# A hybrid block on one core: the local attention's quarters further apart, and longer rows for the ffn's tiles fh and fl

## The chip, the cores and the metric

The kernel runs on one core of one Trainium2 chip. Time is device microseconds of one execution, the lower the better; a run's time is the time of the whole launch, and the profile's span goes from the first to the last instruction of one execution.

## The reference, cut to what matters

A block of three mixers with a feed-forward part made of retrieved experts comes first; then two layers of the form below, on 256 tokens of width 1024, in float32.

```
def hybrid_layer(x, ...):
    h = rms_norm(x, norm1_g)
    za, zb, zc, zd, zg = split(h @ w_in)
    ya = retention(za, ...)            # rotary, decayed scores, group norm
    yb = conformer_conv(zb, ...)       # 31 taps per channel, layer norm
    yc = spatial_gating(zc, ...)
    yd = swa_attention(zd, ...)        # the local attention
    mix = sum over n of sigmoid(gate n) * (y_n @ w_branch[n])
    x = x + mix @ w_out
    h = rms_norm(x, norm2_g)
    gt, up = split(h @ w_ffn_in)       # 2 x 2816 columns
    return x + (silu(gt) * up) @ w_ffn_out

def swa_attention(zd, ...):            # blocks of 128 queries, 2 kv heads, 4 q heads each
    q, k = rms_norm(...), rms_norm(...)
    s = q k^T * d**-0.5 + bias         # keys of the block and of the one before it
    m = max(max(s), sink)
    p = exp(s - m)
    o = (p / (sum(p) + exp(sink - m))) @ v
```

## The kernel before

**Weights.** Every weight matrix is cut into blocks of 128 x 128, stored in the order of use. SyncE loads 16 blocks at a time into "raw"; ScalarE rounds 8 of them to "whi" (line 90) and VectorE, or GpSimd in one stage, makes the remainder "wlo" (line 93). Eight blocks are a slot; there are three slots of each kind, so the two engines work up to three slots ahead of TensorE. A product is three matmuls a block (lines 173 to 175, or 179 to 181 where the activations are the stationary side): high by high, high by low, low by high.

**Tasks.** What is no weight product (the local attention, the retention, the convolution) is a Python generator. `blks` hands out a block and calls `tick` for every two blocks; a task that yields n goes on n slots later (four ticks to a slot). So tasks are strewn between the weight products when the program is written. From that order a planner, which simulates the engines, makes the order of each engine's queue: what was written earlier goes first where its inputs are there. Buffers of one tag (bg and mm in PSUM, four each; w2, seven; T4, thirteen) are given out in the order in which they were written. The remainders and the loads of the weights go ahead of everything else.

**A layer's mixers.** In order: the convolution's input (cc), the local attention's projections dq and dkv, then rq, rk, rv and rg of the retention, gu and gv of the spatial gating, then the four gated branches (first the local attention's, then the retention's, the gating's and the convolution's) and w_out. The convolution's 31 taps for each of four rows of channels (line 1134) run on VectorE, two to a slot, behind the newest remainder.

**The local attention** (`swa`) is four tasks, one for each block of queries n and kv head g, the two quarters with n = 0 (one block of keys) first. Each writes: the scores (line 1229) into two tiles "pss" of the pool bg, their evacuation with the bias (line 1231), maximum, sink and negation (lines 1236 to 1239, VectorE), four exponentials and that of the sink (lines 1241 and 1243, ScalarE), sum, reciprocal and division (lines 1244 to 1246, VectorE); then it yields. After that come the transposes "ptt" (line 1254, the helper's line 243) and their evacuation on ScalarE into a tile of w2 (line 1256), one more slot, and the product with the values "po" (line 1260), which is split into dh and dl (lines 186 and 187). The first branch needs dh and dl at its first product "pp", eight blocks after its start.

**The ffn.** `ffn` keeps silu(gt) * up as two tiles of 22 rows of 256 float32, fh and fl (lines 1453 and 1454). The first product (f_in) fills them, row by row, through `split` (lines 186 and 187). The second (f_out) reads them: in the first layer as the moving side of matmuls with 256 columns (lines 173 to 175, 528 of them), in the second as the stationary side of matmuls with 512 columns (lines 179 to 181, 264 of them).

Of the kernel before, what the change touches and what calls it, by code (L numbers as in the profile page):

```python
# [8 lines left out]
F32R = mybir.dt.float32r  # L9
# [10 lines left out]
P = 128  # L20
S = 256
# [21 lines left out]
FF = 22  # L43
N_BLOCKS = 5416
W_SHAPE = (-(-N_BLOCKS // 16), 128, 2048)
TAPS = 2
N_SCR = 5
LRU_PACE = 5
N_WARM = 50
# [80 lines left out]
class Core:  # L130
# [118 lines left out]
    def scr(self, name):  # L249
        return self.tp.tile([P, S], F32, tag="scr", name=name, bufs=N_SCR)  # L250

# [813 lines left out]
    def mixers(self, l):  # L1065
        tc, nc, a, ws = self.tc, self.nc, self.a, self.ws
        with ExitStack() as st:
            pa = st.enter_context(tc.tile_pool(name=f"a{l}", bufs=1))
            self.pad(pa)
            p = st.enter_context(tc.tile_pool(name=f"m{l}", bufs=1))  # L1070
# [7 lines left out]
            def T4(dt=F32):  # L1078
                return pa.tile([P, 4, S], dt, tag="t4", name="t4", bufs=13)

            def tmp(shape, tag, bufs=2, dt=F32):
                return p.tile(shape, dt, tag=tag, name=tag, bufs=bufs)
# [45 lines left out]
            def conv(bh, bl):  # L1128
                for j in range(4):
                    nc.vector.tensor_scalar(out=cy[:, j, :], in0=up[:, j, 0:S], scalar1=hw[:, j * NT:j * NT + 1],  # L1130
                                            scalar2=cb[:, j:j + 1], op0=ALU.mult, op1=ALU.add)
                    for i in range(1, NT):
                        with tc.issue_after(ws.on_vector):
                            nc.vector.scalar_tensor_tensor(out=cy[:, j, :], in0=up[:, j, i:i + S],
                                                           scalar=hw[:, j * NT + i:j * NT + i + 1], in1=cy[:, j, :],
                                                           op0=ALU.mult, op1=ALU.add)
                        if i % TAPS == 0:
                            yield 1
# [81 lines left out]
            def swa(n, g):  # L1220
                k0 = 0 if n else P
                nk = S - k0
                s = T4()
                for i in range(2):

                    ps = self.bg.tile([P, 2, nk], F32, tag="bg", name="pss")
                    rows = slice(64 * i, 64 * i + 64)
                    for j in range(2):
                        nc.tensor.matmul(ps[:, j, :], lhsT=qT[rows, 2 * g + j, n * P:n * P + P],
                                         rhs=kT[rows, g, 0:nk], start=True, stop=True)  # L1230
                    nc.vector.scalar_tensor_tensor(out=s[:, i:4:2, :nk], in0=ps, scalar=0.125,
                                                   in1=bias[:, 4 * g + i:4 * g + 4:2, k0:S],
                                                   op0=ALU.mult, op1=ALU.add)
                sm = tmp([P, 4, 4], "sm", 3)
                sk = sink[:, 4 * g:4 * g + 4]
                nc.vector.tensor_reduce(out=sm[:, 0, :], in_=s[:, :, :nk], axis=AX.X, op=ALU.max)
                nc.vector.tensor_tensor(out=sm[:, 0, :], in0=sm[:, 0, :], in1=sk, op=ALU.max)
                nc.vector.tensor_tensor(out=sm[:, 2, :], in0=sk, in1=sm[:, 0, :], op=ALU.subtract)
                nc.vector.tensor_scalar(out=sm[:, 0, :], in0=sm[:, 0, :], scalar1=-1.0, scalar2=None, op0=ALU.mult)
                for i in range(4):  # L1240
                    nc.scalar.activation(out=s[:, i, :nk], in_=s[:, i, :nk], func=AF.Exp, bias=sm[:, 0, i:i + 1],
                                         accum_out=sm[:, 1, i:i + 1])
                nc.scalar.activation(out=sm[:, 2, :], in_=sm[:, 2, :], func=AF.Exp)
                nc.vector.tensor_tensor(out=sm[:, 1, :], in0=sm[:, 1, :], in1=sm[:, 2, :], op=ALU.add)
                nc.vector.reciprocal(out=sm[:, 3, :], in_=sm[:, 1, :])
                nc.vector.tensor_tensor(out=s[:, :, :nk], in0=s[:, :, :nk],
                                        in1=sm[:, 3, :, None].to_broadcast([P, 4, nk]), op=ALU.mult)
                yield 3
                nkb = nk // P
                pts = []  # L1250
                for kb in range(nkb):
                    pt = self.bg.tile([P, 4, P], F32, tag="bg", name="ptt")
                    for i in range(4):
                        self.transpose(pt[:, i, :], s[:, i, kb * P:kb * P + P])
                    pts.append(tmp([P, 4, P], "w2", 7))
                    nc.scalar.activation(out=pts[-1], in_=pt, func=AF.Copy)
                yield 1
                po = self.bg.tile([P, 4, P], F32, tag="bg", name="po")
                for kb in range(nkb):
                    nc.tensor.matmul(po, lhsT=vd[:, kb if n else 0, g].rearrange("p a b -> p (a b)"),  # L1260
                                     rhs=pts[kb], start=kb == 0, stop=kb == nkb - 1)
                for i in range(2):
                    rows = slice(64 * i, 64 * i + 64)
                    src = po.rearrange("p (b two) q -> p b two q", two=2)[rows, :, i, :]
                    self.split(dh[rows, 2 * g:2 * g + 2, n * P:n * P + P], dl[rows, 2 * g:2 * g + 2, n * P:n * P + P],
                               src)
# [19 lines left out]
            def ev_rot(d):  # L1286
                def ev(c, ps):
                    nc.scalar.activation(out=d[:, c:c + 2, :], in_=ps, func=AF.Copy)
                    t_rot.append(self.add(rot(d[:, c:c + 2, :])))
                return ev  # L1290
            self.finish(*loads[1])
            self.proj_b(W2["rq"](l), 2, KD, hh, hl, ev_rot(rq))
            self.finish(*t_qk, *loads[0])
            t_swa = [self.add(swa(n, g), 1 + 3 * (2 * n + g)) for n in range(2) for g in range(2)]
            self.proj_b(W2["rq"](l), 4, KD, hh, hl, ev_rot(rq), c0=2)
            self.proj_b(W2["rk"](l), 4, KD, hh, hl, ev_rot(rk))
            rv = T4().rearrange("p a b -> p (a b)").rearrange("p (t c) -> p t c", t=2)
# [150 lines left out]
    def ffn(self, l):  # L1448
        tc, nc, a, ws = self.tc, self.nc, self.a, self.ws
        with ExitStack() as st:  # L1450
            p = st.enter_context(tc.tile_pool(name=f"f{l}", bufs=1))
            self.pad(p)
            fh = p.tile([P, FF, S], F32R, tag="fh", name="fh")
            fl = p.tile([P, FF, S], F32R, tag="fl", name="fl")

            def ev(c, ps):
                j = c // 2
                sg = p.tile([P, S], F32, tag="fsg", name="fsg", bufs=2)
                nc.scalar.activation(out=sg, in_=ps[:, 0, :], func=AF.Silu)
                nc.vector.tensor_tensor(out=sg, in0=sg, in1=ps[:, 1, :], op=ALU.mult)  # L1460
                self.split(fh[:, j, :], fl[:, j, :], sg)
            self.from_lead((f"f_in{l}", 0, 0), 2 * FF, ev)
            if l == 0:
                raw = [tuple(p.tile([P, S], F32R, tag=f"raw{i}", name="raw") for i in (k, 8 + k)) for k in range(KD)]
                g1 = self.pc2(1)
                acc = self.residual(("f_out0", 0, 0), FF, fh, fl, raw, g1)
                self.lead(W2["cc"](1), raw, g1, [acc], lambda ps: self.rsqrt(ps[:, 0, :]), LEAD_C)
                self.dump("x5", self.x)
            else:
                xn = p.tile([P, 2, KD, P], F32, tag="xn", name="xn")  # L1470
                for t in range(2):
                    for g in range(2):
                        pt = self.bg.tile([P, 4, P], F32, tag="bg", name="pxn")
                        for j in range(4):
                            self.transpose(pt[:, j, :], self.x[:, 4 * g + j, t * P:t * P + P])
                        nc.scalar.activation(out=xn[:, t, 4 * g:4 * g + 4, :], in_=pt, func=AF.Copy)
                for g in range(2):
                    def ev_fin(t, ps):
                        o = p.tile([P, 512], F32, tag="fo", name="fo", bufs=3)
                        nc.vector.tensor_tensor(out=o, in0=xn[:, t, 4 * g:4 * g + 4, :].rearrange("p a b -> p (a b)"),  # L1480
                                                in1=ps, op=ALU.add)
                        nc.sync.dma_start(out=self.out[0, t * P:t * P + P, g * 512:g * 512 + 512], in_=o)
                    self.proj_a(("f_out1", 0, 4 * g), FF, 4, fh, fl, ev_fin)
# [139 lines left out]
```

## Time and profile before

| | |
|---|---|
| median of 3 runs | 2127.13 us (2122.9 to 2136.53) |
| the profiled execution | 2123.62 us |
| its span | 2121.8 us |
| instructions | 41452 |
| TensorE busy | 2032.5 us, 96% |
| VectorE busy | 1680.1 us, 79% |
| ScalarE busy | 1164.8 us, 55% |
| GpSimd busy | 252.3 us, 12% |

The engines are called PE (TensorE's matmuls), PEld (its weight loads), DVE (VectorE), ACT (ScalarE), POOL (GpSimd) and SP (SyncE). Matmuls overlap, so the mean duration of one is longer than the distance from one to the next; the pace of a stretch is its length by its number of matmuls. The first layer's mixers lie at about 1180 to 1470 us of the span, its ffn at 1480 to 1650; the second layer's at about 1660 to 1945 and 1960 to 2117.

### The profile page before, as it was taken

Reading aid. Unit: us, or ns where it says so; the run is one execution under the profiler, and the core shown is the slowest. Engines: PE = TensorE matmul, PEld = TensorE weight load, DVE = VectorE, ACT = ScalarE, POOL = GpSimd, SP = SyncE. Lnnn points to the kernel's source line nnn. Section 1 sums busy time; section 2 is a strip of 40 time slices with the busy share of each in tenths; the row PEclk is TensorE's granted clock in tenths of the full one; section 3 lists DMA queues with packets and bytes.
Section 4 is the critical chain, followed back from the end, with each engine's and each line's share of the span. In section 5 each row is a group of like instructions: output and inputs, shape, how many; then the busy total and the mean of one; then the engine's idle time right before and its main releaser. Section 6 shows DMA issues by size and latency. Waiting matters only on the chain.

```text
span 2121.8 us, 41452 instructions
## 1 busy us (share of the span) xinstructions
PE 2032.5 (96%) x16818; PEld 1974.2 (93%) x16818; DVE 1680.1 (79%) x3308; ACT 1164.8 (55%) x1910; POOL 252.3 (12%) x162
## 2 busy tenths in 40 slices
PE   8978999959999999999999989999999999999999
PEld 7958999959999899999999878999999988999997
DVE  7847669998999999996556998977655898977654
ACT  6648754435555455554446656466545657466543
POOL 2101205844000000000000110210000110200000
PEclk9988999979999999999999999999999999999999
DMA  5443554525445444444555642555555643554554
GB/s 209 147 119 124 181 210 168 179 100 178 173 171 177 151 168 179 177 177 163 197 193 185 217 159 100 185 196 178 208 191 197 236 159 120 187 191 179 199 194 154
DMA packets 56923, 370.01 MB, mean 174 GB/s; under 512 B 6491, under 2 KB 10140, under 8 KB 13468
## 3 DMA queue, kind: packets, MB, share of 16 engines
q1 hardware_dynamic: 50256, 357.06, 46.9%
q10 hardware_dynamic: 6476, 10.31, 1.9%
q8 instruction: 131, 2.15, 0.4%
q14 instruction: 60, 0.49, 0.1%
HBM read 364.73 MB, written 2.62 MB: 173 GB/s over the span
## 4 chain that ended last, share of the span: by engine, by line
PE 81%; DVE 9%; issue 3%; DMA 3%; ACT 3%; POOL 1%; ACTq 0%; SPq 0%; POOLq 0%; DVEq 0%
PE mm L175 6%; PE mm L173 6%; PE mm L174 6%; PE acc L174 5%; PE pu L173 5%; PE acc L175 5%; PE acc L173 5%; PE pu L175 5%; PE pu L174 5%; PE pg L175 3%; PE pg L174 3%; PE pg L173 3%; DVE wlo L93 2%; PE mml L173 2%; PE mml L175 2%
## 5 line engine op out<-in xcount | busy, mean ns | idle before, releaser
L90 ACT ACTIVATE whi<-raw 128x1024 fp32r<-128x1024 f32 x677 | 716.9, 1060 | 764.6 <-PE acc L174 170.3
L93 DVE TENSOR_TENSOR wlo<-raw,whi 128x1024 fp32r<-128x1024 f32 x629 | 778.3, 1238 | 323.6 <-ACT whi L90 320.7
L173 PE MATMUL pu<-hh,whi 128*128 128x256 f32 x1024 | 290.5, 284 | 20.3 <-ACT whi L90 20.3
L175 PE MATMUL pu<-hh,wlo 128*128 128x256 f32 x1024 | 287.0, 280 | 3.1 <-POOL wlo L93 3.1
L174 PE MATMUL pu<-hl,whi 128*128 128x256 f32 x1024 | 286.1, 279 | 0.0
L175 PE MATMUL mm<-hh,wlo 128*128 128x256 f32 x1008 | 280.8, 279 | 5.3 <-DVE wlo L93 5.3
L173 PE MATMUL mm<-hh,whi 128*128 128x256 f32 x1008 | 281.6, 280 | 0.0
L174 PE MATMUL mm<-hl,whi 128*128 128x256 f32 x1008 | 280.3, 278 | 0.0
L174 PE MATMUL acc<-ga,whi 128*128 128x256 f32 x1000 | 267.9, 280 | 4.5 <-DVE ga L187 4.4
L175 PE MATMUL acc<-ga,wlo 128*128 128x256 f32 x1000 | 267.3, 279 | 0.0
L173 PE MATMUL acc<-ga,whi 128*128 128x256 f32 x1000 | 242.5, 281 | 5.0 <-ACT ga L186 5.0
L173 PEld LDWEIGHTS pu<-hh,whi 128*128 128x128 f32 x1024 | 194.7, 190 | 20.5 <-ACT whi L90 20.5
L173 PE MATMUL pg<-hh,whi 128*128 128x256 f32 x704 | 199.5, 283 | 12.3 <-ACT lth L552 11.7
L175 PE MATMUL pg<-hh,wlo 128*128 128x256 f32 x704 | 198.4, 282 | 0.6 <-DVE wlo L93 0.5
L175 PEld LDWEIGHTS pu<-hh,wlo 128*128 128x128 f32 x1024 | 194.3, 190 | 3.8 <-POOL wlo L93 3.8
L174 PE MATMUL pg<-hl,whi 128*128 128x256 f32 x704 | 197.7, 281 | 0.0
L175 PEld LDWEIGHTS mm<-hh,wlo 128*128 128x128 f32 x1008 | 190.3, 189 | 7.8 <-DVE wlo L93 6.7
L174 PEld LDWEIGHTS pu<-hl,whi 128*128 128x128 f32 x1024 | 194.0, 189 | 0.0
L174 PEld LDWEIGHTS acc<-ga,whi 128*128 128x128 f32 x1000 | 188.6, 189 | 5.3 <-DVE ga L187 5.3
L174 PEld LDWEIGHTS mm<-hl,whi 128*128 128x128 f32 x1008 | 190.3, 189 | 1.8 <-issue 1.6
L173 PEld LDWEIGHTS mm<-hh,whi 128*128 128x128 f32 x1008 | 190.6, 189 | 1.0 <-issue 0.8
L175 PEld LDWEIGHTS acc<-ga,wlo 128*128 128x128 f32 x1000 | 188.7, 189 | 0.0
(412 smaller groups left out, 4873.4 us busy)
## 6 DMA issues: line engine op xcount, KB each, us to landing
raw<-in_w SPq DMA_DIRECT2D x336, 1024.0 KB, 4.8
raw<-in_w SPq DMA_DIRECT2D x5, 512.0 KB, 7.6
bias<-bias_scr ACTq DMA_DIRECT2D x4, 512.0 KB, 5.4
bias_scr<-sbb ACTq DMA_DIRECT2D x4, 384.0 KB
cl<-in_cstl ACTq DMA_DIRECT2D x2, 576.0 KB, 7.4
x<-in_xT SPq DMA_DIRECT2D x4, 256.0 KB, 5.8
memt<-in_memT ACTq DMA_DIRECT2D x1, 1024.0 KB, 4.8
keys<-in_keysT ACTq DMA_DIRECT2D x1, 1024.0 KB
```

The lines of the kernel that those rows point to most:

```text
L90: self.on_scalar = nc.scalar.activation(out=hi, in_=src, func=AF.Copy).ins
L93: i = eng.tensor_tensor(out=lo, in0=src, in1=hi.bitcast(F32), op=ALU.subtract)
L173: mm(out, lhsT=wh, rhs=xh, start=start, stop=False)
L174: mm(out, lhsT=wh, rhs=xl, start=False, stop=False)
L175: mm(out, lhsT=wl, rhs=xh, start=False, stop=stop)
```

## The change

Two numbers of the local attention become names with other values. The quarters' tasks start 1, 5, 9 and 13 slots after they are added, where they started at 1, 4, 7 and 10; between the softmax and the transposes a quarter yields 5 slots, where it yielded 3. The rows of fh and fl are laid out 272 elements (1088 bytes) apart where they were 256 (1024); what is written and read is still the first 256 of each.

```
+SWA_SOFT, SWA_PACE = 5, 4
+ROW = 272
...
                 nc.vector.tensor_tensor(out=s[:, :, :nk], in0=s[:, :, :nk],
                                         in1=sm[:, 3, :, None].to_broadcast([P, 4, nk]), op=ALU.mult)
-                yield 3
+                yield SWA_SOFT
                 nkb = nk // P
...
-            t_swa = [self.add(swa(n, g), 1 + 3 * (2 * n + g)) for n in range(2) for g in range(2)]
+            t_swa = [self.add(swa(n, g), 1 + SWA_PACE * (2 * n + g)) for n in range(2) for g in range(2)]
...
-            fh = p.tile([P, FF, S], F32R, tag="fh", name="fh")
-            fl = p.tile([P, FF, S], F32R, tag="fl", name="fl")
+            fh = p.tile([P, FF, ROW], F32R, tag="fh", name="fh")[:, :, :S]
+            fl = p.tile([P, FF, ROW], F32R, tag="fl", name="fl")[:, :, :S]
```

## Rows read from the trace of the kernel before

**Rows 1.** The page, busy time, share of the span and instructions of each engine.
```profile
PE 2032.5 (96%) x16818; PEld 1974.2 (93%) x16818; DVE 1680.1 (79%) x3308; ACT 1164.8 (55%) x1910; POOL 252.3 (12%) x162
```
**Rows 2.** The page, the chain that ended last, shares of the span by engine.
```profile
PE 81%; DVE 9%; issue 3%; DMA 3%; ACT 3%; POOL 1%; ACTq 0%; SPq 0%; POOLq 0%; DVEq 0%
```
**Rows 3.** PE's waits: who for whom, us in total, times, longest.
```profile
PE ptt L243 <- DVE t L1246: 11.8, 4, 4.0
...
PE mm L175 <- DVE wlo L93: 5.3, 5, 2.0
```
**Rows 4.** The order of time on PE, first layer: start, length, count, idle before.
```profile
1239.28 0.39 PE L181 MATMUL mm<-wlo,hh 128*128 128x512 f32 x1
...
1255.28 0.63 PE L243 MATMUL ptt<-cst,t 128*128 128x128 f32 x4 [3.09 <-DVE t L1246]
1255.84 1.40 PE L1229 MATMUL pss<-kT,t 64*128 64x256 f32 x8
...
1274.50 1.94 PE L243 MATMUL ptt<-cst,t 128*128 128x128 f32 x8 [3.95 <-DVE t L1246]
...
1278.39 3.00 PE L1260 MATMUL po<-w,vd 128*128 128x512 f32 x4
...
1294.33 1.88 PE L1260 MATMUL po<-w,vd 128*128 128x512 f32 x4
...
1299.66 0.28 PE L173 MATMUL pp<-t,whi 128*128 128x256 f32 x1
```
**Rows 5.** Windows of 10 us: busy time by engine, PEclk (granted clock), DMA.
```profile
1250.00:1260.00 10.00, 6.91 (x39) 4.91 (x38) 9.92 (x20) 5.50 (x14) 0.00 (x0) 0.83 0.55 206
1270.00:1280.00 10.00, 6.05 (x23) 3.96 (x23) 6.72 (x14) 5.81 (x11) 0.00 (x0) 0.68 0.45 171
...
1750.00:1760.00 10.00, 9.40 (x38) 6.49 (x39) 6.43 (x14) 7.80 (x17) 0.00 (x0) 0.83 0.28 107
```
**Rows 6.** The order of time on DVE, the third quarter's first and last instruction.
```profile
1258.50 0.69 DVE L1231 SCALAR_TENSOR_TENSOR t<-pss,bias 128x512 f32<-128x512 f32 x1
...
1273.13 1.22 DVE L1246 TENSOR_TENSOR t<-t,sm 128x1024 f32<-128x1024 f32 x1
```
**Rows 7.** The order of time on ACT: evacuations of transposes, rv and rg.
```profile
1255.94 0.60 ACT L1256 ACTIVATE w<-ptt 128x512 f32<-128x512 f32 x1 [2.26 <-PE ptt L243]
1256.44 1.08 ACT L1300 ACTIVATE t<-mm 128x512 f32<-128x512 f32 x2
...
1277.03 0.59 ACT L1306 ACTIVATE w<-mm 128x512 f32<-128x512 f32 x1
```
**Rows 8.** Windows in which PE never waits, columns as in rows 5.
```profile
220.00:310.00 90.00, 90.00 (x766) 90.00 (x766) 61.09 (x86) 57.86 (x85) 15.85 (x15) 1.00 0.55 199
1366.00:1390.00 24.00, 24.00 (x206) 24.00 (x205) 22.35 (x34) 11.34 (x16) 7.80 (x7) 1.00 0.57 210
1402.00:1438.00 36.00, 36.00 (x320) 36.00 (x319) 26.79 (x43) 23.18 (x40) 1.49 (x2) 1.00 0.52 183
1500.00:1580.00 80.00, 80.00 (x709) 80.00 (x708) 45.72 (x60) 39.57 (x59) 0.00 (x0) 1.00 0.54 193
1582.00:1641.00 59.00, 59.00 (x523) 59.00 (x522) 33.51 (x42) 29.77 (x38) 0.00 (x0) 1.00 0.54 191
2058.00:2117.00 59.00, 59.00 (x260) 48.40 (x259) 26.53 (x24) 21.39 (x22) 0.00 (x0) 1.00 0.48 167
```
**Rows 9.** Windows of the two layers' local attention, columns as in rows 5.
```profile
1214.00:1300.00 86.00, 77.99 (x496) 66.46 (x495) 76.73 (x138) 47.61 (x89) 8.32 (x5) 0.94 0.40 148
1695.00:1776.00 81.00, 75.97 (x503) 65.79 (x502) 74.43 (x135) 48.13 (x89) 7.14 (x4) 0.98 0.43 153
```
**Rows 10.** Groups by line and shape: the remainder's writes to fl.
```profile
L187 DVE TENSOR_TENSOR fl<-fsg,fh 128x256 fp32r<-128x256 f32 x44 | 18.2, 419 | 0.1
```
**Rows 11.** The order of time on DVE: the fourth quarter's last split.
```profile
1298.62 0.43 DVE L187 TENSOR_TENSOR t<-po,t 64x256 fp32r<-64x256 f32 x1
```

## The prediction

> **What bounds the kernel now.** I read the page's busy shares first: TensorE (PE) is busy 96% of the span, VectorE (DVE) 79% [rows 1]. The chain that ended last is 81% PE and 9% DVE [rows 2]. So time is won only where PE stands still or runs slowly, and 2121.8 us of span leave some 89 us of idle PE. The list of PE's waits says which of it the change can reach: "ptt" waiting for DVE's line 1246, four times, 11.8 us, the longest 4.0 [rows 3]. That is the local attention: the transposes wait for the softmax. The larger waits on that list lie in other stages and stay.
>
> The order of time shows the shape. In the first layer PE stands for 3.09 us before the second quarter's transposes (1255.28) and 3.95 us before the third's (1274.50) [rows 4]. The second layer does the same at two places. Each stop costs more than its length: the granted clock is 0.83 in 1250 to 1260, 0.68 in 1270 to 1280, and 0.83 in 1750 to 1760 of the second layer [rows 5], a share of these stretches being run at 1.2 GHz and not 2.4 (four matmuls of po at 1278.39 take 3.00 us, at 1294.33 1.88) [rows 4]. As lost full-speed time that is 10 x (0.17 + 0.32 + 0.17) = 6.6 us. Stops and clock together are 18.4 us, the most that the first part of the change can give back by this count.
>
> Why does the softmax come late? In the third quarter DVE reads the first scores at 1258.50 and ends its ninth instruction, the division, at 1274.35 [rows 6]: 15.9 us for nine instructions of 0.15 to 1.22 us, since DVE also makes weight remainders (L93) and convolution taps (L1134), and is 99% busy from 1250 to 1260 [rows 5]. And why does PE stop instead of taking other matmuls? It can only run as far ahead as the four buffers of the pool mm reach. ScalarE (ACT) empties rv's two buffers at 1256.44, directly behind the evacuation of the second quarter's transposes at 1255.94, though the last matmul of rv started at 1239.28; rg's first buffer is emptied at 1277.03, behind the third quarter's, which start at 1274.50 [rows 4, 7]. So two buffers are held by rv, two are filled by rg, and PE has no buffer left exactly where it stops.
>
> **The change, part by part: the local attention.** A slot is 8 weight blocks, 24 matmuls; at 709 matmuls in 80 us [rows 8] it is 24 x 112.8 ns = 2.71 us. From the code: a quarter counts ticks of two blocks from the task's start. Before, scores are written into the program at blocks 6, 30, 54, 78 after the start and transposes at 30, 54, 78, 102; each group of transposes stands in the same tick as the next quarter's scores and ahead of them. After, scores stand at 6, 38, 70, 102 and transposes at 46, 78, 110, 142; blocks 16 to 47 are rk, 48 to 79 rv, 80 to 111 rg, 112 to 143 gu. No instruction is added or removed; two things move.
>
> First, each softmax gets 5 slots (13.6 us) in place of 3 (8.1), 5.4 us more, which is longer than each of the four stops (at most 4.0). And the next quarter's scores come one slot ahead of these transposes, not behind them, so that DVE can start on them while the older softmax ends.
>
> Second, what is queued behind the transposes on ACT changes. The second quarter's transposes are now written after rv's evacuation (block 78 is only reached at the tick of block 80), so rv's two buffers come free without them and PE gets 32 blocks, 10.8 us, more before it has to stop. The third quarter's (block 110) come after rg's first evacuation and ahead of the second alone. This is what I count on most: where the sum of DVE work still makes a softmax late, PE has matmuls to run.
>
> What limits the gain is DVE. From 1214 to 1300 it is busy 76.73 of 86 us, in the second layer's 1695 to 1776 74.43 of 81 [rows 9]. None of its work goes, so these stretches can shrink by at most 9.3 + 6.6 = 15.9 us unless taps slide behind them. DVE's slack now lies where the two later quarters run (1270 to 1280: 6.72 of 10 busy [rows 5]), and the new places put softmax work there. I take three quarters of 15.9, 12 us: the dependencies of four softmaxes will not let DVE run without a gap, and the tail of the last quarter is little shortened. The ends: 0 (all waits come back as waits for the weights' remainder, 5.3 us of which stand in the list already [rows 3]) and 18.4.
>
> Moved past: the last quarter's product (po) goes from block 106 to 146 and the retention's first score blocks (from block 118) now run between the quarters, in the same PSUM pool bg. They wait for nobody on the path: the retention's result is first needed one branch, 12 slots, after the local attention's. No DMA is moved. Cost 0; if bg's order held the retention up, its 12 slots (32 us) cover it.
>
> **The ffn's rows.** fh and fl have 22 rows each; rows of 1088 bytes make each tile 1,408 bytes longer and shift what lies behind. No instruction changes in count or shape. Touched are 44 ACT and 44 DVE writes (fl 419 ns each [rows 10]), which lie beside matmuls (DVE is busy 45.72 of 80 us in the ffn's first product [rows 8]): cost 0, and even 10% on them would not show. Then the second products: 528 matmuls of 256 columns in the first layer, 264 of 512 in the second, whose operand rows move.
>
> Their price the trace does not show, so I bound it. PE knows two paces that hold for long: 766 matmuls in 90 us (117.5 ns) in 220 to 310, and 523 in 59 us (112.8) in the second product itself [rows 8]. The slow one is 4.2% more: over both stages (528 x 112.8 ns = 59.6 us; 260 matmuls in 59 us are 226.9 ns, x 264 = 59.9 us) +5.0 us. On the other side no stretch is faster than 112.5 (320 in 36 us, 1402 to 1438), which would give -0.2. The pitch is not what separates the paces: the same loop over the same tiles runs at 116.5 (206 in 24 us, 1366 to 1390) and at 112.5 [rows 8]. So I take 0.
>
> A rule weighs against that zero. The Trainium skill ("TensorE: Matmul & The Clock Gate", section Back-to-back issue gap) gives 262 cycles for 256 columns and 518 for 512. At 2.4 GHz that is an estimate of 109.2 and 215.8 ns; if the pitch were what stands between, the stages would give 528 x 3.6 ns + 264 x 11.1 ns = 4.8 us, and the sum would be 2110. No stretch of this trace reaches that page's gap, at any tile.
>
> **Sum.** 2123.6 us (the profiled execution) - 12 - 0 = 2111.6. That execution is 3.5 us below the median of the three runs (2127.1), so against the median: **2115 us**, 0.6% faster. The three runs spread over 13.6 us (0.6%); about 1% is what a measurement of this kernel can tell from no change.
>
> **Rivals.** *DVE is the bound and the waits only move* (for: 99% busy before the stops; against: its slack behind them). PE then waits for wlo in place of ptt, and what is left is part of the clock, some 3 us: 2124. *All of it goes*, 18.4 us, taps sliding into the gated stage: 2109; for it, the taps have until the fourth branch; against it, DVE is busy 22.35 of 24 us there (1366 to 1390) [rows 8]. *The end of the attention becomes the wait.* Today the last split ends at 1299.05 and the first matmul that needs it starts at 1299.66; po starts at 1294.33, 4.7 us before the split's end [rows 4, 11]. After, po stands at block 146 and the need at 184, 38 blocks or 12.9 us, so the last softmax may be 8.2 us late. The third's ran 18.7 us from scores to transposes (1255.84 to 1274.50 [rows 4]), 5.1 over 5 slots; twice that is 2.0 over the margin, with some clock 3 per layer: 2121.
>
> *Slower: the pace flips.* The paces change at stops of PE and then hold. The change moves every stop of the mixers, and behind them lie some 570 us now run at the fast pace (branches, w_out, both ffn products of both layers, 1300 to 1650 and 1778 to 2057 less what is slow already). All of it slow costs 4.2%, 24 us: 2115 + 24 = 2139; the point at which it eats the gain is 12 / 0.042 = 286 us of slow stretch. For it: the slow stretch of 90 us above; against it: the ffn's stretches are at 112.8 today, or at twice that with 512 columns [rows 8]. *The pitch sets the pace of the second products* (place: the two stages, 119.5 us; price: up to +5.0 by the rows, if the new rows bring the slow pace): 2120.
>
> **How the numbers follow.** Forecast 2111 to 2119: 0.44. Waits move (2124): 0.20. All goes (2109): 0.12. The end waits (2121): 0.08. The pace flips: 0.10, half of it to about 2128, half beyond. The pitch acts (2120): 0.04. The change does nothing that shows (2127): 0.02. The range 2104 to 2131 takes in all but the worse half of the pace and the spread of the runs. Faster by over 1% (under 2105.9) needs all of the gain and a fast median: 0.09. Slower by over 1% (over 2148.4) needs nearly all of the pace's price and more: 0.04. Within 1%: 0.87.
>
> **What would show it.** PE's list: ptt on L1246 under 3 us of the 11.8; granted clock 1.00 through both layers' local attention. On ACT, rv's evacuation ahead of the second quarter's, PE's scores one slot ahead of the transposes. The stretch from the first scores (1214.4) to the branch's first product (1299.66) shorter by 6 to 8 us, the second layer's by 4 to 6. DVE busy over 93% of it. The ffn's second products still 59 to 60 us each. I am wrong if wlo waits of several us stand there instead, if the last quarter's split holds the first branch, or if the stretches behind show 117 ns per matmul.

## The result, and the profile after

The changed kernel takes 2113.41 us (median of 20 runs, 2106.61 to 2122.47), the kernel before 2124.36 (median of 20 runs beside them). One of the latter runs took 7548.94 us and is left out of the ratio. The ratio is 0.9946, 95% interval 0.9932 to 0.9960: 11.5 us faster, with 8.5 to 14.4 as the interval. The forecast was 12 us. The profiled execution took 2114.22 us, span 2112.4, where the sum had 2111.6. The total came out; two of its terms did not, and they nearly cancel, which is luck.

The page's busy times [rows 1] and the chain [rows 2], after:

```profile
PE 2036.2 (96%) x16818; PEld 1978.7 (94%) x16818; DVE 1678.1 (79%) x3308; ACT 1158.7 (55%) x1906; POOL 251.1 (12%) x162
...
PE 80%; DVE 9%; ACT 4%; issue 3%; DMA 3%; POOL 1%; ACTq 0%; SPq 0%; POOLq 0%; DVEq 0%
```

Every line number is 2 higher than before. The four fewer ACT instructions are table loads (58 before, 54 now); the other engines' counts are the same. PE's waits after, against [rows 3]: "ptt" no longer stands in the list at all, and the waits for DVE's remainder grew from 5.3 and 1.5 to these:

```profile
PE mm L177 <- DVE wlo L95: 5.6, 5, 2.0
...
PE mm L183 <- DVE wlo L95: 4.4, 6, 1.2
...
PE po L1262 <- ACT w L1258: 0.6, 1, 0.6
...
PE prs L1318 <- DVE rsc L1322: 0.3, 1, 0.3
```

So 11.8 us went and about 4 came back elsewhere, 3.2 of them as waits for the remainder. The windows of the local attention, with the columns of [rows 5, 9]: three of 10 us, then the two layers' stretches.

```profile
1250.00:1260.00 10.00, 9.44 (x75) 8.12 (x74) 9.91 (x16) 3.73 (x6) 1.47 (x1) 1.00 0.29 105
...
1270.00:1280.00 10.00, 10.00 (x46) 7.69 (x45) 8.67 (x14) 9.13 (x19) 0.00 (x0) 1.00 0.48 190
...
1750.00:1760.00 10.00, 10.00 (x53) 8.17 (x52) 9.64 (x20) 6.34 (x9) 0.00 (x0) 1.00 0.29 105
...
1214.00:1290.00 76.00, 73.13 (x491) 63.17 (x492) 73.70 (x134) 46.12 (x87) 7.04 (x4) 1.00 0.43 153
1692.00:1767.00 75.00, 72.72 (x491) 63.23 (x490) 72.02 (x142) 45.11 (x86) 7.17 (x4) 1.00 0.42 147
```

The granted clock is 1.00 in all of them (0.83, 0.68 and 0.83 before), and DVE is busy 73.70 of 76 and 72.02 of 75 us, 97% and 96%, where it had 89% and 92% [rows 9]. The order of time on PE and on ACT, first layer:

```profile
1222.59 0.72 PE L1231 MATMUL pss<-kT,t 64*128 64x128 f32 x8
...
1241.91 0.60 PE L245 MATMUL ptt<-cst,t 128*128 128x128 f32 x4
...
1246.27 1.14 PE L1231 MATMUL pss<-kT,t 64*128 64x256 f32 x8
...
1289.40 0.28 PE L175 MATMUL pp<-t,whi 128*128 128x256 f32 x1
```
```profile
1246.66 1.06 ACT L1302 ACTIVATE t<-mm 128x512 f32<-128x512 f32 x2
...
1252.76 0.60 ACT L1258 ACTIVATE w<-ptt 128x512 f32<-128x512 f32 x1
1253.26 0.59 ACT L1308 ACTIVATE w<-mm 128x512 f32<-128x512 f32 x1
```

The second quarter's scores (1222.59) now stand ahead of the first quarter's transposes (1241.91), and rv's evacuation (line 1302) ahead of the second quarter's (line 1258), both as forecast. The branch's first product starts 75.5 us after the first scores, where it took 85.2 before, and 77.8 in the second layer, where it took 82.6: 9.8 and 4.7 us less, with 6 to 8 and 4 to 6 forecast; it even starts ahead of the last po (1290.71), on blocks that are ready. Last, the first layer's ffn (its first product, its second) and the second layer's second product, against [rows 8]:

```profile
1500.00:1575.00 75.00, 75.00 (x639) 75.00 (x638) 41.57 (x53) 35.87 (x54) 0.00 (x0) 1.00 0.52 188
1577.00:1636.00 59.00, 59.00 (x503) 59.00 (x502) 32.37 (x40) 28.29 (x37) 0.00 (x0) 1.00 0.51 180
2048.00:2107.00 59.00, 59.00 (x256) 47.97 (x256) 26.54 (x24) 21.30 (x22) 0.00 (x0) 1.00 0.46 163
```

Here is what the forecast did not have: 75 us by 639 are 117.4 ns per matmul and 59 by 503 are 117.3, where before both products ran at 112.8. The last one does 256 in 59 us where it did 260.

**Where the time went.** All kernels below issue 16818 matmuls, so I count them from 0 in the trace and compare the time from one number to another. Matmuls 9600 to 10200 hold the first layer's local attention ("stretch 1"), 13200 to 14100 the second's ("stretch 2"); "out 1" and "out 2" are the second products of the two layers' ffn, from their first to their last matmul.

```
matmuls               before   after    difference
0 to 9600            1198.95  1198.11   -0.84
9600 to 10200          97.93    88.56   -9.37   stretch 1
10200 to 11700        174.36   174.27   -0.09
11700 to 13200        170.12   176.58   +6.46   ffn, first layer (out 1: 59.73, then 62.16)
13200 to 14100        133.85   129.03   -4.82   stretch 2
14100 to 16500        275.09   273.66   -1.43
16500 to the last      66.32    67.03   +0.71   out 2
```

The stretches of the attention gave 14.2 us, the first layer's ffn took 6.5 back.

### The profile page after: what moved, and what is told of

Its sections match the earlier page's. It is cut to its first block, busy times and chain, and to the rows that moved or that the text cites. A ratio compares the mean times of both kernels' runs of the same rounds, so it can differ in the third digit from the quotient of the medians.

```text
span 2112.4 us, 41444 instructions
## 1 busy us (share of the span) xinstructions
PE 2036.2 (96%) x16818; PEld 1978.7 (94%) x16818; DVE 1678.1 (79%) x3308; ACT 1158.7 (55%) x1906; POOL 251.1 (12%) x162
## 4 chain that ended last, share of the span: by engine, by line
PE 80%; DVE 9%; ACT 4%; issue 3%; DMA 3%; POOL 1%; ACTq 0%; SPq 0%; POOLq 0%; DVEq 0%
PE mm L177 6%; PE mm L175 6%; PE mm L176 6%; PE acc L175 6%; PE acc L176 6%; PE acc L177 5%; PE pu L175 5%; PE pu L177 5%; PE pu L176 5%; PE pg L177 3%; PE pg L175 3%; PE pg L176 3%; DVE wlo L95 2%; PE mml L177 2%; PE mml L175 2%
```

## The experiments

All results in one table; us, ratios against the kernel before with 95% intervals. "ptt" is PE's wait for the division.

```
kernel            stretch 1  stretch 2   ptt    out 1   out 2   ratio
before               97.93    133.85    11.8    59.73   60.20
after                88.56    129.03     0      62.16   60.91   0.9946 (0.9932 to 0.9960)
e1 attention         89.23    128.95     0      59.73   60.20   0.9914 (0.9882 to 0.9946)
e2 rows              98.94    133.85    12.1    62.15   60.91   1.0022 (1.0001 to 1.0042)
e3 starts            98.14    136.40    10.7    59.73   60.20   1.0003 (0.9978 to 1.0028)
e4 softmax           88.86    129.09     0      59.73   61.37   0.9969 (0.9945 to 0.9992)
e5 offset            98.31    135.24    12.2    62.06   61.14   1.0042 (1.0018 to 1.0066)
e6 pitch             95.16    135.11    12.3    62.36   60.86   1.0026 (0.9993 to 1.0059)
e7 row 288           98.22    133.82    12.1    61.48   61.14   1.0002 (0.9982 to 1.0022)
e8 again             88.05    129.00     0      62.15   60.91   one run, 2117.46 us
e9 rv by DVE         93.49    134.98     5.7    59.73   60.20   0.9994 (0.9974 to 1.0013)
e10 rv late          87.25    129.24     0      62.07   60.20   0.9927 (0.9902 to 0.9953)
e11 behind          101.14    134.39    12.0    59.73   60.20   0.9998 (0.9977 to 1.0019)
e12 no taps          86.17    126.53     0.9    59.73   60.20   one run, 2100.26 us
```

Six of these (before, e2, e5, e6, e7, e11) have every queue in the same order; their stretch 1 runs from 95.16 to 101.14 and their stretch 2 from 133.82 to 135.24, so much does one execution differ from another. The three with the changed attention in the same order (after, e1, e8) lie at 88.05 to 89.23 and 128.95 to 129.03. By the means, 98.3 to 88.6 and 134.4 to 129.0, the attention is worth 15.1 us.

A stretch by number does not hold quite the same matmuls where the order of PE's queue is another: e4's and e12's stretch 1 have 12 and 10 of 512 columns fewer than that of before. From 9600 to 10360, and from 13200 to 14232, every kernel has issued the same ones:

```
                  9600 to 10360   13200 to 14232
before                117.38          149.29
after                 108.68          144.40
e1 attention          109.34          144.31
e3 starts             118.36          151.77
e4 softmax            110.00          145.76
e10 rv late           107.36          144.61
e12 no taps           105.69          141.67
```

By the means of the same six and three kernels this gives the attention 14.5 us.

**The two parts alone.** e1 has the attention's numbers and rows of 1024 bytes, e2 the kernel before with wide rows:

```
e1:  yield 3 -> yield 5;  1 + 3 * (2 * n + g) -> 1 + 4 * (2 * n + g)
e2:  fh = p.tile([P, FF, 272], F32R, tag="fh", name="fh")[:, :, :S]     (and fl)
```

> The attention's part alone: starts four slots apart and five slots before the transposes; the rows of fh and fl stay 1024 bytes apart. Theory A (the attention gives the gain; the slow pace of the first layer's ffn is a matter of where TensorE's last stops fall, the pitch has nothing to do with it): the time between the same matmuls shrinks by 9.4 us in the first layer's mixers and by about 5 in the second's, as in the changed kernel, no wait for the division stays, and the ffn of the first layer, with the same stops ahead of it, is again at about 118 ns per matmul; ratio 0.995. Rival B (the 1088-byte rows bring the slow pace): the same gain in the mixers, but the ffn's first layer is at 113.3 ns, so that the 6.5 us which the changed kernel loses there are kept; ratio 0.992. Rival C (the rows give a part of the gain): ratio 0.997 or above.

> The rows alone: fh and fl with rows 1088 bytes apart, the attention as before, every queue in the order of the kernel before. Theory A (rows cost nothing): ratio 1.000, the ffn's products of the first layer at 113.3 ns per matmul and both second products within 0.3 us of before. Rival B (these rows bring the slow pace): the first layer's ffn at about 118 ns, 6.5 us longer, and the second product of the second layer 0.7 us longer as in the changed kernel; ratio 1.003. Rival C (the rows are faster): second products 2 us or more shorter together, ratio 0.998 or less.

The windows of e1 (first product, out 1, out 2), then of e2 (first product, out 1):

```profile
1495.00:1570.00 75.00, 75.00 (x664) 75.00 (x663) 42.79 (x55) 37.38 (x56) 0.00 (x0) 1.00 0.54 190
1571.00:1630.00 59.00, 59.00 (x523) 59.00 (x522) 33.61 (x41) 29.52 (x38) 0.00 (x0) 1.00 0.54 191
2041.00:2100.00 59.00, 59.00 (x260) 48.40 (x259) 26.52 (x24) 21.57 (x22) 0.00 (x0) 1.00 0.48 167
```
```profile
1503.00:1578.00 75.00, 75.00 (x664) 75.00 (x663) 42.98 (x56) 36.87 (x55) 0.00 (x0) 1.00 0.54 195
1581.00:1640.00 59.00, 59.00 (x503) 59.00 (x502) 32.52 (x40) 28.27 (x38) 0.00 (x0) 1.00 0.51 181
```

e1 is at 113.0 and 112.8 ns through both products, e2 at 113.0 in the first and 117.3 in the second. So the rows do cost, by the profiles: 62.15 - 59.73 = 2.4 us in out 1 and 60.91 - 60.20 = 0.7 in out 2, 3.1 together, and e2's ratio agrees (1.0001 to 1.0042). My own theory A, which gave the rows nothing, falls. Rival B is right for the second product and not for the first, which e2 runs fast. Where e2 changes its pace is seen on PE in order of time:

```profile
1579.71 0.28 PE L173 MATMUL mm<-hh,whi 128*128 128x256 f32 x1
1579.82 0.28 PE L174 MATMUL mm<-hl,whi 128*128 128x256 f32 x1
1579.94 0.28 PE L175 MATMUL mm<-hh,wlo 128*128 128x256 f32 x1
1580.05 0.28 PE L173 MATMUL mm<-fh,whi 128*128 128x256 f32 x1
...
1580.39 0.28 PE L173 MATMUL mm<-fh,whi 128*128 128x256 f32 x1
...
1580.75 0.28 PE L173 MATMUL mm<-fh,whi 128*128 128x256 f32 x1
...
1581.10 0.28 PE L173 MATMUL mm<-fh,whi 128*128 128x256 f32 x1
```

Three matmuls take 0.34 us up to the first that reads fh (1579.71 to 1580.05) and in the first block of fh (1580.39), then 0.36 and 0.35. No wait stands there: the slow pace comes with the operands.

**The attention's two numbers apart.** e3 changes the starts, e4 the softmax's slots:

```
e3:  1 + 3 * (2 * n + g) -> 1 + 4 * (2 * n + g)
e4:  yield 3 -> yield 5
```

> Only the starts: four slots apart, three slots before the transposes as before. Scores are then written at blocks 6, 38, 70, 102 and transposes at 30, 62, 94, 126. Theory A, as the prediction put it (buffers: TensorE stops when the four buffers of mm are full, and what counts is that rv's evacuation is written ahead of the second quarter's transposes): here they still stand ahead of it, TensorE can reach block 111 before it needs them, and its scores come 8 blocks later, so the stops stay: waits for the division of 10 to 16 us, the two mixers at most 3 us shorter, ratio 0.998 to 1.001. Rival (what counts is that VectorE's work is spread wider): the waits fall under 5 us and the mixers are 8 us or more shorter; ratio about 0.996. The pace of the stretches behind may add or take up to 6 us in any of these kernels, so the mixers' own length decides.

> Only the time for the softmax: five slots in place of three, starts three apart as before. Scores are written at blocks 6, 30, 54, 78 and transposes at 46, 70, 94, 118, so the next quarter's scores stand ahead of the transposes, but rv's evacuation (block 80) still stands behind the second quarter's and rg's first (block 96) behind the third's. Theory A (buffers, as in the prediction): TensorE can still reach only block 111 before the second quarter's transposes, so the stops stay nearly as before: 8 to 12 us of waits for the division, ratio 0.998 to 1.000. Rival (the softmax's own slots and the scores' place ahead of the transposes are what counts): waits under 3 us, the mixers shorter by 10 us or more in sum, ratio 0.995.

The starts alone give nothing: e3 keeps 10.7 us of waits in two stops, the longer of them here.

```profile
1259.47 1.09 PE L243 MATMUL ptt<-cst,t 128*128 128x128 f32 x4 [6.65 <-DVE t L1246]
```

The softmax's slots alone give most of it: e4 has no wait for the division, and its stretches look like those of the changed kernel. Counted over the same matmuls it gains 7.4 and 3.5 us where e1 gains 8.0 and 5.0, so with the longer softmax the starts may add some 2 us. Theory A (buffers) had no gain in e4, and falls in that form. In e4's order of time the second quarter's scores (1223.28) again stand ahead of the first quarter's transposes (1244.88): with starts three apart and five slots for the softmax, two softmaxes are under way at once. In e3, as before, there is one at a time (its second scores start at 1238.32, its first transposes at 1232.10). More slots and this order come together here; no run parts them.

e4's ratio (0.9969) is worse than its stretches, and worse than e1's (0.9914). Its profile has 640 matmuls in 75 us (117.2 ns) of the second layer's first product, with rows of 1024 bytes:

```profile
1970.00:2045.00 75.00, 75.00 (x640) 75.00 (x638) 40.91 (x54) 36.00 (x53) 0.00 (x0) 1.00 0.54 190
```

That is the profiled execution; whether it holds in the other eleven, and so accounts for the ratio, no trace shows.

**What about the rows.** Four kernels with other layouts, or the same program once more:

```
e5:  fh = p.tile([P, FF * S + 352], ...)     fl 1408 bytes further, rows 1024 bytes
e6:  fh = p.tile([P, FF * 272 + 160], ...)   rows 1088 bytes, fl 24576 bytes behind fh
e7:  rows of 288 elements (1152 bytes)
e8:  the changed kernel, unaltered
```

> The kernel before with the rows of fh and fl 1024 bytes apart as they were, but 1408 bytes left free behind fh, so that fl and all behind it lie where the 1088-byte rows put them. Every queue in the order of before. Theory D (the distance between rows brings the slow pace of the first layer's second product, 118 ns in place of 113.3, as with the rows alone): here 113.3 ns, 59.7 us for the product, ratio 1.000. Rival E (the place of fl against fh, or of what lies behind, brings it): 118 ns, 62.2 us, ratio 1.002. Rival F (neither, the pace is drawn anew in each execution): either, and the other stretches change pace too.

> The kernel before with rows 1088 bytes apart, and 640 bytes left free behind fh so that fl begins 24,576 bytes behind it, again at a multiple of 2048. Every queue in the order of before. Theory D (distance between rows): 118 ns in the first layer's second product, 62.2 us, and the second layer's 0.7 us longer as with the rows alone; ratio 1.002. Rival E (place of fl against fh): 113.3 ns, ratio 1.000. Rival F (drawn anew): either.

> The kernel before with rows 1152 bytes apart (288 elements), a multiple of 128 bytes where 1088 is one of 64 only. Every queue in the order of before. Theory D1 (any distance other than 1024 brings the slow pace): 118 ns in the first layer's second product, the second layer's 0.7 us longer; ratio 1.002. Theory D2 (the odd multiple of 64 brings it): 113.3 ns, 59.7 us, ratio 1.000. Rival F (drawn anew): either.

> The changed kernel once more, to see which paces of its profile come back. If the paces are set by the program (addresses and order), the first layer's ffn is again at 118 ns per matmul through both products, 6.5 us longer than before, and all stretches ahead of it have the paces of the first profile. If they are drawn in each execution, some stretches come out at the other pace, and the first product of this ffn, whose operands the rows don't touch, is one of them at even odds, while the second product (touched by the rows) stays at 118.

Out 1 in e5, then e6, then e7:

```profile
1591.00:1650.00 59.00, 59.00 (x503) 59.00 (x502) 32.27 (x40) 28.40 (x36) 0.00 (x0) 1.00 0.53 181
```
```profile
1578.00:1637.00 59.00, 59.00 (x500) 59.00 (x500) 32.54 (x40) 28.08 (x38) 0.00 (x0) 1.00 0.53 179
```
```profile
1593.00:1652.00 59.00, 59.00 (x508) 59.00 (x507) 32.54 (x40) 28.95 (x38) 0.00 (x0) 1.00 0.52 184
```

All three are slow: 117.3, 118.0 and 116.1 ns. So it isn't the distance between rows alone (e5 keeps 1024 bytes) nor the odd multiple of 64 (e7), nor fl's place at a multiple of 2048 bytes (e6 has one). D, D2 and E each fail as the one cause; each of these layouts is slow. e5's ratio (1.0042) is the worst and e7's (1.0002) the best of the three, which out 1 and out 2 do not explain.

e8 shows the rest. Its first product:

```profile
1500.00:1575.00 75.00, 75.00 (x664) 75.00 (x663) 43.00 (x55) 37.25 (x56) 0.00 (x0) 1.00 0.55 197
```

The same program that ran this product at 117.4 ns runs it at 113.0 in another execution, while its out 1 is again at 62.15 us. So of the 6.5 us that the changed kernel's profile lost in this ffn, 4.0 (first product) were this execution's, and 2.4 are the program's. The same kind of change shows ahead of the attention, where matmuls 0 to 9600 take between 1196.8 (e10) and 1210.2 us (e7). Of the four kernels with the changed order of PE's queue two ran the first product slowly (after, and e10 below), of the six in the order of before none did; these are too few to say whether the new order makes it likelier.

**What lies behind fl.**

```
e11:  fl = p.tile([P, FF * S + 704], ...)    fh and fl in place, what is behind 2816 bytes further
```

> The kernel before with 2816 bytes left free behind fl, so that fh and fl lie where they lay, with rows of 1024 bytes, and only what lies behind them moves as far as with the 1088-byte rows. Every queue in the order of before. Theory H (the slow pace of the first layer's second product comes from where its operands' rows lie): 113.3 ns per matmul, 59.7 us, ratio 1.000. Rival I (from the tiles behind, which ScalarE and VectorE write meanwhile): 118 ns, 62.2 us, ratio 1.002 to 1.003.

```profile
1591.00:1650.00 59.00, 59.00 (x523) 59.00 (x523) 33.54 (x42) 29.73 (x38) 0.00 (x0) 1.00 0.53 190
```

Fast, out 1 at 59.73: with PE's operands in place the pace stays, so it is where they lie, not what ACT and DVE write meanwhile.

**Buffers, or two softmaxes at once.** e9 is the kernel before with rv emptied by DVE; e10 is e1 with rv's evacuation three slots later:

```
e9:   nc.vector.tensor_copy(out=rv[:, t, :], in_=ps)
e10:  def rv_late(t, ps):
          yield 3
          nc.scalar.activation(out=rv[:, t, :], in_=ps, func=AF.Copy)
```

> The kernel before with one thing changed: rv's two buffers are emptied by VectorE and not by ScalarE (two copies of about 0.6 us a layer more on VectorE), so that they come free without standing behind the evacuation of the second quarter's transposes. The transposes still stand ahead of the next quarter's scores. Theory A of the prediction (TensorE stops because rv holds two of four buffers): the stop before the second quarter's transposes goes, the waits for the division fall from 11.8 to under 6 us, and the same matmuls take 4 to 7 us less in the first layer's stretch (97.93 before) and 2 to 3 in the second's (133.85). Rival G (what counts is that the next quarter's scores come ahead of the transposes, so that two softmaxes are under way at once): waits of 10 to 13 us, both stretches within 1.5 us of before, ratio 1.000.

> The changed attention (starts four slots apart, five to the transposes, rows as before) with rv's evacuation held back by three slots, so that on ScalarE it stands behind the second quarter's transposes and behind rg's first buffer; two buffers of mm are held as in the kernel before, or longer. Scores still come ahead of the transposes. Theory A (buffers): the stop comes back, 5 us or more of waits for the division or for buffers in the first layer, stretch 94 us or more where the attention alone had 89.23 (second layer 132 or more against 128.95). Rival G (two softmaxes at once): waits for the division under 2 us, the stretches within 1.5 us of 89.23 and 128.95, ratio 0.991 to 0.996.

e9 doesn't do what it was made for. On DVE the copies stand no earlier than they did on ACT (1256.44 [rows 7]):

```profile
1260.40 1.28 DVE L1300 COPY t<-mm 128x512 f32<-128x512 f32 x2
```
```profile
PE ptt L243 <- DVE t L1246: 5.7, 3, 3.1
...
PE mm L173 <- DVE t L1300: 4.2, 2, 4.0
```

A wait for a buffer takes the place of half of the wait for the division, and the ratio is that of no change. Theory A's bounds were met in part (5.7 us of waits, and 4.4 us less in stretch 1), but stretch 2 is 1.1 us longer, and the buffers did not come free earlier. It says nothing on the question. e10 does: on PE, DVE and GpSimd its order is that of e1, on ACT it differs in 12 places. ACT's order there, first layer:

```profile
1250.11 0.60 ACT L1256 ACTIVATE w<-ptt 128x512 f32<-128x512 f32 x1
1250.60 0.59 ACT L1310 ACTIVATE w<-mm 128x512 f32<-128x512 f32 x1
1251.08 1.09 ACT L1301 ACTIVATE t<-mm 128x512 f32<-128x512 f32 x2
```

rv (line 1301) is emptied behind the second quarter's transposes and behind rg's first buffer, and yet there is no wait for the division and the stretches are 87.25 and 129.24. So rv's place on ACT is not what the gain hangs on; rival G has it (stretch 1 is even 2.0 us shorter than e1's, where it allowed 1.5). e10's out 1 is slow (62.07) behind a first product that was slow too (640 in 75 us), with rows in place: the slow pace is also carried from one product into the next. The weight loads tell this pace from that of the layouts. First after's first product, then out 1 of e10, e2 and e7:

```profile
L176 PEld LDWEIGHTS mm<-hl,whi 128*128 128x128 f32 x213 | 40.9, 192 | 0.0
```
```profile
L174 PEld LDWEIGHTS mm<-fl,whi 128*128 128x128 f32 x167 | 32.1, 192 | 0.0
```
```profile
L174 PEld LDWEIGHTS mm<-fl,whi 128*128 128x128 f32 x167 | 31.6, 189 | 0.0
```
```profile
L174 PEld LDWEIGHTS mm<-fl,whi 128*128 128x128 f32 x169 | 31.7, 188 | 0.0
```

The loads of the other two matmuls of a block take 188 ns in all four, 187 once. So one load in three takes 192 ns in the pace that comes and goes, and none does by the mean in the pace of the layouts.

**Is it DVE?**

```
e12:  i > 1 or nc.vector.scalar_tensor_tensor(out=cy[:, j, :], ...)
```

> The kernel before without 29 of the 30 added taps of each of the convolution's rows of channels in both layers' mixers: 116 VectorE instructions of about 0.48 us a layer are left out, and the output with them. Theory of the prediction (the softmax is late since VectorE is full): waits for the division fall from 11.8 to under 4 us, the waits for the weights' remainder in these stretches go too, and the first layer's stretch falls from 97.93 to 85 to 89 us, the second's from 133.85 to 126 to 129. Rival G (one softmax at a time, a chain of small instructions through two engines, is too long by itself): waits of 7 us or more stay, stretches of 93 us or more and 131 us or more.

```profile
PE ptt L243 <- DVE t L1246: 0.9, 1, 0.9
```
```profile
1214.00:1291.00 77.00, 76.15 (x525) 67.24 (x522) 58.21 (x93) 44.38 (x86) 8.68 (x5) 1.00 0.44 155
```

With DVE busy 58.21 of 77 us, one softmax at a time and rv's evacuation behind, as in the old order, run with one stop of 0.9 us at a clock of 1.00. (The planner's order of the queues is not that of before in every place.) DVE's fullness is the cause, as the prediction said; two softmaxes at once are a cure for it. Over the same matmuls the changed kernel is 3.0 and 2.7 us above this one.

## Why the prediction was right, and where it wasn't

**What bounds it.** Right. The four stops were softmaxes kept waiting by a full DVE (e12), and the clock's dips were theirs: with the stops gone the granted clock is 1.00.

**"What I count on most".** Wrong. rv's evacuation did move ahead of the second quarter's transposes, but e10 moves it back and loses nothing. The buffers say how far PE can run on; by the order of time the new kernel doesn't have to run that far, since the divisions end earlier (the second quarter's transposes start at 1249.17, 1255.28 before). What counts is the step that the prediction named first and in passing: five slots, with the next quarter's scores ahead of these transposes (e4). The starts four apart, half of the change's first part, give nothing of their own (e3). Whether the slots or the order would do it alone is not shown.

**The attention's size, 12 us.** Too small: 14.2 in the profile, 15.1 by the means. The term was three quarters of DVE's idle 15.9 us, on the ground that four softmaxes would not let DVE run without a gap. With two under way at once DVE is 97% and 96% busy, but the idle time is not what was sized too small. From the first scores to the branch's first product, in both layers, before and then after:

```profile
1214.43:1299.66 85.23, 77.22 (x489) 65.85 (x489) 76.26 (x138) 47.29 (x88) 7.89 (x5) 0.94 0.40 146
1695.19:1777.74 82.55, 77.52 (x517) 67.51 (x517) 75.61 (x137) 49.64 (x91) 7.14 (x4) 0.98 0.42 149
```
```profile
1213.92:1289.40 75.48, 72.61 (x489) 62.83 (x489) 73.18 (x132) 45.73 (x86) 7.11 (x5) 1.00 0.43 155
1691.37:1769.18 77.81, 75.53 (x518) 65.94 (x517) 74.33 (x151) 47.89 (x90) 7.17 (x4) 1.00 0.41 145
```

DVE's idle time falls from 8.97 + 6.94 = 15.9 us to 2.30 + 3.48 = 5.8. That is 10.1 us, under two thirds; the other 4.4 of these 14.5 us are DVE work that slid behind the stretch (3.1 and 1.3), into time in which DVE had stood idle: up to matmuls 10360 and 14232 its work is the same within 0.4 us, and its idle time falls from 26.6 to 13.4. The step that failed is "unless taps slide behind them": the prediction named it and put nothing for it in the 12. About 3 us came back as waits for the remainder; the rival in which all of it comes back did not happen. The end of the attention held nobody: no "pp" stands in PE's list.

**The rows, 0 us.** Wrong: +3.1, inside the bounds (-0.2 to +5.0); the first layer's second product did not stay at 59 to 60 us. The argument was that the same loop over the same tiles runs at either pace [rows 8], so the layout is not what separates them. The observation holds (e8, e4), the conclusion doesn't: a pace may be drawn in one product and be set by the operands' place in another. The slow stretch that priced the bound (220 to 310) is of the drawn kind, one load in three at 192 ns, so that the price of the layout's pace came out near it is luck. That rival ("the pitch sets the pace", 0.04) is what happened, beside the gain, though the pitch alone isn't its cause. The Trainium skill's rule ("TensorE: Matmul & The Clock Gate", Back-to-back issue gap), whose estimate would have given 4.8 us back here, is not borne out: no ffn product here ran faster than 112.8 ns for 256 columns or 226.9 for 512.

**The pace flips.** Its premise, that the pace changes at stops and then holds, is half right: it holds through a product, but e2 changes it without a stop. In the profiled execution one product came out slow (+4.0 us), which e8 did not repeat; the branches and w_out (-0.09) and what lies behind the second stretch (-1.43) lost nothing.

**The sum**, for the profiled execution: 2123.6 - 14.2 (attention) + 3.1 (rows) + 4.0 (the draw) - 2.4 (the rest of the table) = 2114.1, measured 2114.2. The forecast 2111.6 had a gain too small by 2.2, nothing for the rows and nothing for the draw. The total was right by luck, since these partly cancel.

The best ratio is that of the attention without the rows: e1, 2107.01 us, 0.9914. Its interval touches that of the changed kernel, and the two were not timed side by side; the profiles put the rows at 3.1 us, so they are better left out. What stays open: which rule of addresses makes out 1 slow (every layout tried but that of before and e11 did), what sets the draw, and why e4's ratio lags behind e1's.

## What to carry to other kernels

Where a full vector engine makes a chain of small steps late, write the next chain's start ahead of the first one's end, so that two are under way: the engine's gaps go (89% to 97% busy) though its work stays. Price it by two terms: the part of that engine's idle time in the stretch that goes (10.1 of 15.9 us here), and the work that can slide behind the stretch (4.4 us here). And time each half of a change alone: here one half gave about 14 us, the other took 3, and the whole looked like the forecast.

## What the runs showed of the hardware

TensorE's float32r products of 256 columns hold a pace of some 113 ns or one of 116 to 118 for a whole product of 60 to 110 us, at a granted clock of 1.00 and with no wait. A first product of the ffn came out at either in two executions of one program (639 and 664 matmuls in 75 us); in its slow pace one weight load in three takes 192 ns and not 188. A second product was set by where its moving operand lay in SBUF: 59.73 us, or 61.48 to 62.36 in four other layouts (and 62.07 once in the first layout, in e10, behind a slow first product). In e2 the step comes within two blocks of the first operand that lies elsewhere. A pad of 1408 bytes between two tiles is enough, one of 2816 behind both does nothing. Products of 512 columns, with the same rows as the stationary side, lose less: 60.20 to between 60.86 and 61.14 (61.37 in e4, with the rows of before, behind a slow first product).
